# One softmax chain rewritten: queries times -1/8, the sink as one more column of the scores, a minimum for the maximum

## The chip, the core and the metric

The kernel runs on one core of a Trainium2 chip. The metric is the device time of one execution in microseconds (us); the time of a kernel is the median of its runs. The core has five engines with queues of their own: TensorE (PE in the profile, with its weight loads as PEld), VectorE (DVE), ScalarE (ACT), GpSimd (POOL) and SyncE (SP), which here issues most transfers.

## What is computed

One layer of a diffusion backbone on 1024 tokens of width 1024, with 256 context tokens: a modulated RMSNorm, then eight heads of windowed attention beside a short convolution, an output projection, and a mixture of 16 experts that each choose 128 tokens. The part that matters here is the attention's softmax, over one sink per head, all context keys and the keys within 128 positions:

```python
s_loc = jnp.einsum('bnqkgd,bnjkd->bnkgqj', qb, kb).astype(jnp.float32) * scale     # scale = 1/8
s_ctx = jnp.einsum('bnqkgd,bjkd->bnkgqj', qb, k_ctx).astype(jnp.float32) * scale
s_loc = jnp.where(valid[None, :, None, None], s_loc, -jnp.inf)
sk = jnp.broadcast_to(sink..., s_loc.shape[:-1] + (1,))
p = jax.nn.softmax(jnp.concatenate([sk, s_ctx, s_loc], axis=-1), axis=-1)
out = p_ctx @ v_ctx + p_loc @ v_loc        # the sink's share has no value
```

## The kernel before

All products that need precision are made of three: each operand is split into a high part (a cast on ScalarE) and a low part (a subtraction on VectorE or GpSimd).

The order of TensorE's instructions is the order in which the program writes them. For the other engines a planner chooses the order when the kernel is built, by a clock of its own; it may run an instruction long before the place where it is written. Some late parts of the kernel fix more engines by hand.

The stages in order: modulation and context; keys and values; the projection of the queries, tile by tile of 128 tokens (`q_proj`, line 496, and `q_turn`), woven with `mod_stream`, which sums further modulation rows on GpSimd; then the attention woven with the convolution; the output projection with the routing; the experts.

In `q_proj` a tile of queries is rotated (`rotary`, lines 328 to 335), split by L510 (high, ScalarE) and L511 (low, VectorE) into `qs`, and turned on TensorE in `q_turn` (L521).

The attention has 32 units: 8 blocks of 128 queries times 4 pairs of heads. `scores(u)` does a unit in two halves, one head each: two pairs of matmuls (L564 for the context keys, L566 for the window) into `ps_s`; one VectorE operation (L576) that adds the mask, writes the scores to `sm` in SBUF and gives the row's maximum with 8 times the sink (`sink8`) as the start; L578, that maximum times -1/8; and L579, the exponential on ScalarE with its sum `esum`. After the second half come the shares: L586 adds sink and negative maximum, L587 takes the exponential, L588 adds the sums, L589 takes the reciprocal for both heads at once, and the scores are multiplied by it, one head on ScalarE (L593) and one on VectorE (L595). A unit of blocks 1 to 6 has five key blocks (640 columns), one of blocks 0 and 7 four (512).

`values(u - 1)` is written between and behind the halves of `scores(u)`: it turns the shares of the unit before on TensorE, two key blocks at a time (L623), splits them (L626 high on ScalarE, L627 low on VectorE) and multiplies them with the values (L614). A unit of five key blocks has three such groups: two of 512 columns and one of 256. The last L614 of a unit need all of them. L640 and L644 take the result out.

The pair of score rows lies in one of the 21 slots of SBUF that the program hands out. During the attention the list of free slots is nearly empty, and the scores take turns in two of them, each free once the unit that held it has been turned.

The convolution's matmuls (L731 to L733) stand between those of the attention, three at a time. Beside them, ScalarE casts its weights (L711) and GpSimd subtracts (L712); and after a part of the convolution GpSimd multiplies (L756) and adds (L761, twice) the taps, which ScalarE scales (L760).

Of the kernel before, what the change touches and what calls it, by code (L numbers as in the profile page):

```python
# [9 lines left out]
F32 = mybir.dt.float32  # L10
# [3 lines left out]
AF = mybir.ActivationFunctionType  # L14
OP = mybir.AluOpType
# [6 lines left out]
NH = 8  # L22
# [4 lines left out]
NT = S // 128  # L27
# [3 lines left out]
NEG = -1.0e30  # L31
# [55 lines left out]
def tile_layer(ctx, tc, x, c, cx, c_ctx, w_ada, b_ada, g_mix, w_in, conv_w, sink, w_out, g_ffn,  # L87
               w_router, w_gate, w_up, w_down, g_final, rope, amask, ident_in, triu_in, iota_in, out):
    nc = tc.nc
    consts = ctx.enter_context(tc.tile_pool(name="consts", bufs=1))  # L90
# [5 lines left out]
    slots = Slots(big, NSLOT)  # L96
# [12 lines left out]
    def w4(name, shape=(1024,), dtype=F32, tag="w4"):  # L109
        return shaped(work.tile([128, 1026 if dtype != BF else 2052], dtype, tag=tag, bufs=NW4, name=name), shape)  # L110
# [4 lines left out]
    def p2(i, name):  # L115
        return psum.tile([128, 2, 512], F32, tag=f"P{i}", name=name)

    def p1(i, name):
        return psum.tile([128, 512], F32, tag=f"C{i}", name=name)
# [154 lines left out]
    sinkb = consts.tile([128, NH], F32, name="sinkb")  # L274
    sink8 = consts.tile([128, NH], F32, name="sink8")
    nc.sync.dma_start(sinkb, sink.partition_broadcast(128).rearrange("p o h -> p (o h)"))
    nc.vector.tensor_scalar(sink8, sinkb, 8.0, None, op0=OP.mult)

    def hT_slots(n, name):
        return [slots.get((4, n), F32R, name + a) for a in ("h", "l", "h", "l")]  # L280
# [19 lines left out]
    def hl(hT, k, tok):  # L300
        g, kk = divmod(k, 4)
        return hT[2 * g][0][:, kk, tok], hT[2 * g + 1][0][:, kk, tok]
# [193 lines left out]
    def q_proj(t):  # L496
        half, i = divmod(t, 4)
        ps = p2(1, "ps_q")[:, 0] if t % 2 else p1(3, "ps_q")
        for k in range(KC):
            hi, lo = hl(hT[half], k, slice(i * 128, (i + 1) * 128))  # L500
            g, kk = divmod(k, 4)
            mm(ps, hi, wq[g][0][0][:, kk], start=k == 0, stop=False)
            mm(ps, hi, wq[g][1][0][:, kk], start=False, stop=False)
            mm(ps, lo, wq[g][0][0][:, kk], start=False, stop=k == KC - 1)
            yield 0.65
        t1 = rotary([ps], t, 1, 8)

        qs = w4("qs", (8, 2, HD), F32R)
        tv = t1.rearrange("p (h d) -> p h d", d=HD)
        nc.scalar.copy(qs[:, :, 0, :], tv)  # L510
        nc.vector.tensor_tensor(qs[:, :, 1, :], tv, qs[:, :, 0, :].bitcast(F32), op=OP.subtract)  # L511
        qs_of[t] = qs

    def q_turn(t):
# [24 lines left out]


    attT = {}
    negm = consts.tile([128, NT, NH], F32, name="negm")
    mx = consts.tile([128, NT, NH], F32, name="mx")
    esum = consts.tile([128, NT, NH], F32, name="esum")
    rec = consts.tile([128, NT, NH], F32, name="rec")
    prob = {}

    def geometry(b):
        blocks = [t for t in (b - 1, b, b + 1) if 0 <= t < NT]
        return blocks, 128 * (2 + len(blocks))  # L550

    def scores(u):

        b, hp = divmod(u, 4)
        kv = hp // 2
        blocks, W = geometry(b)
        loc = slice(blocks[0] * 128, (blocks[-1] + 1) * 128)
        sm2, s_sm = slots.get((2, 640), F32, "sm")
        for i in range(2):
            h = 2 * hp + i  # L560
            ps = p2(0, "ps_s")
            st = qT[b // 2][0][:, b % 2, h]
            for a in range(2):
                mm(ps[:, 0, 256:512], st, KCx[:, a, kv, :], start=a == 0, stop=a == 1)  # L564
            for a in range(2):
                mm(ps[:, 1, 0:W - 256], st, KX[a][:, kv, loc], start=a == 0, stop=a == 1)  # L566
            sm = sm2[:, i, :W]
            src = ps.rearrange("p a b -> p (a b)")[:, 256:256 + W]
            dst = sm
            if b == 0:  # L570

                mk = maskt.rearrange("p (a b) -> p a b", a=2)[:, :, 0:256]
                dst, src = [v.rearrange("p (a b) -> p a b", a=2) for v in (sm, src)]
            else:
                mk = maskt[:, 0:W]
            nc.vector.tensor_tensor_reduce(dst, src, mk, op0=OP.add, op1=OP.max, scale=1.0,  # L576
                                           scalar=sink8[:, h:h + 1], accum_out=mx[:, b, h:h + 1])
            nc.vector.tensor_scalar(negm[:, b, h:h + 1], mx[:, b, h:h + 1], -0.125, None, op0=OP.mult)  # L578
            nc.scalar.activation(sm, sm, AF.Exp, bias=negm[:, b, h:h + 1], scale=0.125,  # L579
                                 accum_out=esum[:, b, h:h + 1])  # L580
            if i == 0:
                yield

        hs = slice(2 * hp, 2 * hp + 2)
        r = rec[:, b, hs]
        nc.vector.tensor_tensor(r, sinkb[:, hs], negm[:, b, hs], op=OP.add)  # L586
        nc.scalar.activation(r, r, AF.Exp)  # L587
        nc.vector.tensor_tensor(r, r, esum[:, b, hs], op=OP.add)  # L588
        nc.vector.reciprocal(r, r)  # L589
        for i in range(2):  # L590
            share = rec[:, b, 2 * hp + i:2 * hp + i + 1]
            if i:
                nc.scalar.activation(sm2[:, i, :W], sm2[:, i, :W], AF.Copy, scale=share)  # L593
            else:
                nc.vector.tensor_scalar(sm2[:, i, :W], sm2[:, i, :W], share, None, op0=OP.mult)  # L595
        prob[u] = (sm2, s_sm)
# [480 lines left out]
    i = todo.index(("g", NE - 1, 3))  # L1077
# [391 lines left out]
def _constants():  # L1469
    import ml_dtypes  # L1470
    t = np.arange(S)
    nf = HD // 4
    inv = (np.float32(10000.0) ** (-np.arange(nf, dtype=np.float32) / np.float32(nf))).astype(np.float32)
    ang = np.concatenate([(t // 64).astype(np.float32)[:, None] * inv, (t % 64).astype(np.float32)[:, None] * inv], -1)
    cs, sn = np.cos(ang).astype(np.float32), np.sin(ang).astype(np.float32)
    tab = np.stack([cs, sn, -sn], 1)
    rope = np.ascontiguousarray(tab.reshape(NT, 128, 3, 32).transpose(1, 0, 2, 3)).astype(np.float32)
    q = np.arange(128)[:, None]
    j = np.arange(128)[None, :]
    amask = np.zeros((128, 768), np.float32)  # L1480
    amask[:, 256:384] = np.where(j >= q, 0.0, NEG)
    amask[:, 512:640] = np.where(j <= q, 0.0, NEG)
    amask = amask.astype(ml_dtypes.bfloat16)
    ident = np.eye(128, dtype=np.float32)
    triu = np.triu(np.ones((128, 128))).astype(ml_dtypes.bfloat16)
    iota = np.concatenate([np.broadcast_to(np.arange(1, 129), (128, 128)),
                           np.arange(128)[:, None] + 128 * np.arange(NT)[None, :]], 1).astype(np.float32)
    return {"rope": rope, "amask": amask, "ident_in": ident, "triu_in": triu, "iota_in": iota}
# [28 lines left out]
```

## Time and profile before

| | us |
|---|---|
| median of 3 runs | 1169.38 |
| lowest and highest run | 1166.91, 1170.52 |
| the profiled execution | 1168.05 |
| its span, first to last instruction | 1166.3 |
| TensorE busy in it | 1061.0 (91%) |
| VectorE, ScalarE, GpSimd busy | 966.0, 765.4, 353.3 |

The span is read by stretches. From 110 to 177 us the queries are projected, from 177 to 418 us attention and convolution run together, from 442 us the output projection, from some 580 us the experts. The table by stretches gives each engine's busy time and the number of its instructions, then the granted clock, the share of time in which the transfer engines worked, and GB/s. The view in order of time gives start, length, engine, line, operation, output and inputs, shapes and count; behind it in brackets how long the engine had been idle and what ended that. A matmul's length reaches over the start of the next one, since they are pipelined.

### The profile page before, as it was taken

What the parts mean: (1) busy time and instruction counts of PE and PEld (TensorE: products, weight loads), DVE (VectorE), ACT (ScalarE), POOL (GpSimd) and SP (SyncE); (2) the same over time, 40 slices, a digit from 0 to 9 for tenths busy, and PEclk for the clock granted to TensorE, in tenths of its full rate; (3) what the DMA queues carried; (4) which work ended last, traced back from release to release, by engine and by line L of the source; (5) the groups of instructions that cost most, each with busy time, mean ns of one, the idle gap of its engine ahead of it and who ended that gap; (6) DMA issues with size and microseconds to landing.
All of it is one profiled execution on the core that took longest, in us unless ns stands there. A gap on an engine that the chain in (4) does not pass through costs nothing.

```text
span 1166.3 us, 15621 instructions
## 1 busy us (share of the span) xinstructions
PE 1061.0 (91%) x5486; PEld 875.6 (75%) x5486; DVE 966.0 (83%) x1661; ACT 765.4 (66%) x1057; POOL 353.3 (30%) x294
## 2 busy tenths in 40 slices
PE   6787889999899998998299999999999999999982
PEld 2675667888788877887188888888888888888861
DVE  7787455887878785489889999999999999999975
ACT  7566655766666743222178788778788778888853
POOL 0457681312203131221303333313333312330022
PEclk9797999999999998999599999999999999999996
DMA  9644540100101188657589999999999999999555
GB/s 375 231 163 144 164 145 20 37 19 1 55 1 37 31 307 293 163 142 267 225 295 353 410 393 390 391 390 387 407 394 387 390 391 386 403 398 391 219 182 233
DMA packets 90502, 291.84 MB, mean 250 GB/s; under 512 B 7012, under 2 KB 20784, under 8 KB 89400
## 3 DMA queue, kind: packets, MB, share of 16 engines
q1 hardware_dynamic: 84808, 270.40, 60.7%
q0 software_dynamic: 5616, 20.45, 7.2%
q8 instruction: 43, 0.70, 0.2%
q14 instruction: 35, 0.29, 0.1%
HBM read 266.69 MB, written 24.13 MB: 249 GB/s over the span
## 4 chain that ended last, share of the span: by engine, by line
PE 71%; DVE 11%; DMA 7%; ACT 4%; issue 4%; POOL 2%; POOLq 0%; ACTq 0%; DVEq 0%; SPq 0%
PE pg L1284 14%; PE pu L1284 14%; PE py L1284 13%; PE po L879 6%; PE ps_cv L732 3%; PE ps_cv L731 3%; PE ps_cv L733 3%; PE pt L623 2%; PE po_att L614 2%; DMA xt<-in_x_dram 2%; PE ps_s L566 2%; PE xTp L1270 1%; DVE whl L1133 1%; PE ps_s L564 1%; PE hTtp L1270 1%
## 5 line engine op out<-in xcount | busy, mean ns | idle before, releaser
L1133 DVE TENSOR_TENSOR whl<-raw,whl 128x1024 fp32r<-128x1024 f32 x384 | 455.2, 1224 | 30.5 <-ACT whl L1130 19.6
L1130 ACT CAST whl<-raw 128x1024 fp32r<-128x1024 f32 x384 | 400.2, 1054 | 101.1 <-PE pu L1284 35.7
L1284 PE MATMUL pg<-whl,xT 128*128 128x512 f32 x768 | 187.1, 396 | 2.1 <-DVE whl L1133 2.1
L1284 PE MATMUL pu<-whl,xT 128*128 128x512 f32 x768 | 180.9, 392 | 0.0
L1284 PEld LDWEIGHTS pg<-whl,xT 128*128 128x128 f32 x768 | 142.9, 189 | 31.9 <-DVE whl L1133 2.9
L1284 PE MATMUL py<-whl,hTt 128*128 128x512 f32 x720 | 165.8, 389 | 0.0
L1284 PEld LDWEIGHTS pu<-whl,xT 128*128 128x128 f32 x768 | 143.0, 188 | 29.5
L1284 PEld LDWEIGHTS py<-whl,hTt 128*128 128x128 f32 x720 | 135.1, 188 | 28.4 <-DVE whl L1133 0.3
L1249 POOL TENSOR_SCALAR oh<-iota,pos 128x128 bf16<-128x128 f32 x108 | 106.7, 1002 | 13.3 <-DVE pos L1234 12.8
L1342 POOL DMA_INDIRECT acc_d<-yt,idx x15 | 38.4, 2560 | 195.9 <-DVE yt L1330 195.9
L731 PE MATMUL ps_cv<-hTh,wcs 128*128 128x512 f32 x192 | 81.6, 425 | 0.0
L1294 POOL DMA_INDIRECT xr<-h_d,idx x16 | 21.7, 1357 | 188.8 <-DVE gate_w L1260 188.8
L464 POOL TENSOR_TENSOR acc<-acc,wmod 128x1024 f32<-128x1024 f32 x28 | 69.4, 2494 | 26.4 <-ACT wmod L462 25.9
L626 ACT CAST pth<-pt 128x512 fp32r<-128x512 f32 (+1 forms) x88 | 46.1, 524 | 46.3 <-PE pt L623 46.2
L733 PE MATMUL ps_cv<-hTh,wcs 128*128 128x512 f32 x192 | 76.3, 397 | 0.0
L732 PE MATMUL ps_cv<-hTl,wcs 128*128 128x512 f32 x192 | 76.2, 397 | 0.0
L879 PE MATMUL po<-woh,ah 128*128 128x512 f32 x240 | 71.3, 407 | 0.6 <-ACT woh L224 0.6
L627 DVE TENSOR_TENSOR pth<-pt,pth 128x512 fp32r<-128x512 f32 (+1 forms) x88 | 53.9, 613 | 20.1 <-ACT pth L626 19.2
L712 POOL TENSOR_TENSOR wcs<-wcr,wcs 128x1024 fp32r<-128x1024 f32 x12 | 28.6, 2389 | 110.0 <-ACT wcs L711 87.4
L579 ACT ACTIVATE sm<-sm,negm 128x640 f32<-128x640 f32 (+1 forms) x64 | 51.6, 807 | 4.4 <-DVE negm L578 4.3
L576 DVE CUSTOM_DVE_ANT_0 sm<-ps_s,maskt,sink 128x640 f32<-128x640 f32 (+1 forms) x56 | 48.3, 863 | 6.9 <-PE ps_s L566 6.3
L879 PEld LDWEIGHTS po<-woh,ah 128*128 128x128 f32 x240 | 44.6, 193 | 9.5 <-ACT woh L224 1.0
(285 smaller groups left out, 1821.6 us busy)
## 6 DMA issues: line engine op xcount, KB each, us to landing
raw<-in_w_gate_dram SPq DMA_DIRECT2D x64, 1024.0 KB, 10.1
raw<-in_w_up_dram SPq DMA_DIRECT2D x64, 1024.0 KB, 8.1
raw<-in_w_down_dram SPq DMA_DIRECT2D x64, 1024.0 KB, 10.4
wmod<-in_w_ada_dram SPq DMA_DIRECT2D x32, 512.0 KB, 3.8
wa<-in_w_ada_dram SPq DMA_DIRECT2D x8, 1024.0 KB, 9.5
wcr<-in_w_in_dram SPq DMA_DIRECT2D x12, 512.0 KB, 4.2
xt<-in_x_dram SPq DMA_DIRECT2D x4, 1024.0 KB
wor<-in_w_out_dram SPq DMA_DIRECT2D x4, 1024.0 KB
```

The source lines that it names most:

```text
L464: nc.gpsimd.tensor_tensor(acc, acc, wt, op=OP.add)
L576: nc.vector.tensor_tensor_reduce(dst, src, mk, op0=OP.add, op1=OP.max, scale=1.0, scalar=sink8[:, h:h + 1], accum_out=mx[:, b, h:h + 1])
L579: nc.scalar.activation(sm, sm, AF.Exp, bias=negm[:, b, h:h + 1], scale=0.125, accum_out=esum[:, b, h:h + 1])
L627: nc.vector.tensor_tensor(pth[:, 1, :n], pt[:, :n], pth[:, 0, :n].bitcast(F32), op=OP.subtract)
L731: mm(ps, wsp[:, 0, k], hi, start=k == 0, stop=False)
L732: mm(ps, wsp[:, 0, k], lo, start=False, stop=False)
L733: mm(ps, wsp[:, 1, k], hi, start=False, stop=k == KC - 1)
L879: mm(po[n], a, wo[k // 4, n][j][:, k % 4], start=first, stop=last)
L1130: nc.scalar.copy(w[:, 0], t[:, k % 2])
L1133: low = nc.vector.tensor_tensor(w[:, 1], t[:, k % 2], w[:, 0].bitcast(F32), op=OP.subtract)
L1249: nc.gpsimd.tensor_scalar(oh[:, t], iota1, pos[:, t, 0, e:e + 1], None, op0=OP.is_equal)
L1284: mm(ps[n], a_hl[:, a, k], w[:, j, n * 512:(n + 1) * 512], start=first, stop=last)
```

## The change

The queries are multiplied by -1/8 when they are split, so that the matmuls give the negative of the scaled scores. The masked places get a large positive number, the reduction takes the minimum and starts from minus the sink, and its result is the bias of the exponential as it stands (factor -1). The sink is one more column of the scores: GpSimd copies minus the sink of both heads behind the last column before the reduction, and the exponential and its sum take that column along. So the sum is the whole denominator: L578, L586, L587 and L588 go, and the reciprocal reads `esum`. The slot's rows are 648 long instead of 640.

```diff
-    nc.vector.tensor_scalar(sink8, sinkb, 8.0, None, op0=OP.mult)
+    nc.vector.tensor_scalar(sink8, sinkb, -1.0, None, op0=OP.mult)
...
-        nc.scalar.copy(qs[:, :, 0, :], tv)
-        nc.vector.tensor_tensor(qs[:, :, 1, :], tv, qs[:, :, 0, :].bitcast(F32), op=OP.subtract)
+        nc.scalar.activation(qs[:, :, 0, :], tv, AF.Copy, scale=-0.125)
+        nc.vector.scalar_tensor_tensor(qs[:, :, 1, :], tv, -0.125, qs[:, :, 0, :].bitcast(F32), op0=OP.mult,
+                                       op1=OP.subtract)
...
-        sm2, s_sm = slots.get((2, 640), F32, "sm")
+        sm2, s_sm = slots.get((2, 648), F32, "sm")
+        nc.gpsimd.tensor_copy(sm2[:, :, W], sink8[:, 2 * hp:2 * hp + 2])
...
-            nc.vector.tensor_tensor_reduce(dst, src, mk, op0=OP.add, op1=OP.max, scale=1.0,
+            nc.vector.tensor_tensor_reduce(dst, src, mk, op0=OP.add, op1=OP.min, scale=1.0,
                                            scalar=sink8[:, h:h + 1], accum_out=mx[:, b, h:h + 1])
-            nc.vector.tensor_scalar(negm[:, b, h:h + 1], mx[:, b, h:h + 1], -0.125, None, op0=OP.mult)
-            nc.scalar.activation(sm, sm, AF.Exp, bias=negm[:, b, h:h + 1], scale=0.125,
+            sx = sm2[:, i, :W + 1]
+            nc.scalar.activation(sx, sx, AF.Exp, bias=mx[:, b, h:h + 1], scale=-1.0,
                                  accum_out=esum[:, b, h:h + 1])
...
-        r = rec[:, b, hs]
-        nc.vector.tensor_tensor(r, sinkb[:, hs], negm[:, b, hs], op=OP.add)
-        nc.scalar.activation(r, r, AF.Exp)
-        nc.vector.tensor_tensor(r, r, esum[:, b, hs], op=OP.add)
-        nc.vector.reciprocal(r, r)
+        nc.vector.reciprocal(rec[:, b, hs], esum[:, b, hs])
...
-    amask[:, 256:384] = np.where(j >= q, 0.0, NEG)
-    amask[:, 512:640] = np.where(j <= q, 0.0, NEG)
+    amask[:, 256:384] = np.where(j >= q, 0.0, -NEG)
+    amask[:, 512:640] = np.where(j <= q, 0.0, -NEG)
```

## Rows read from the trace of the kernel before

**Rows 1.** The page's chain that ended last: shares of the span by engine.

```profile
PE 71%; DVE 11%; DMA 7%; ACT 4%; issue 4%; POOL 2%; POOLq 0%; ACTq 0%; DVEq 0%; SPq 0%
```

**Rows 2.** The table by stretches: the attention with the convolution, in one row.

```profile
177.00:418.00 241.00, 233.67 (x1402) 201.47 (x1403) 184.42 (x503) 160.71 (x342) 48.20 (x20) 0.99 0.12 37
```

**Rows 3.** In order of time: one quiet unit of five key blocks, second half.

```profile
259.21 0.60 PE L623 MATMUL pt<-ident,sm 128*128 128x128 f32 x4
...
259.52 0.08 DVE L576 DVE_READ_ACCUMULATOR2_ANT mx<- 128x1 f32 x1
...
259.64 0.15 DVE L578 TENSOR_SCALAR negm<-mx 128x1 f32<-128x1 f32 x1
...
259.84 0.59 ACT L626 CAST pth<-pt 128x512 fp32r<-128x512 f32 x1 [0.95 <-PE pt L623]
...
260.32 0.83 ACT L579 ACTIVATE sm<-sm,negm 128x640 f32<-128x640 f32 x1
...
260.46 0.69 DVE L627 TENSOR_TENSOR pth<-pt,pth 128x512 fp32r<-128x512 f32 x1 [0.48 <-ACT pth L626]
...
261.06 0.19 ACT L579 ACTIVATION_READ_ACCUMULATOR sm<-sm,negm 128x1 f32 x1
261.15 0.19 ACT L587 ACTIVATE rec<-rec 128x2 f32<-128x2 f32 x1
261.24 0.36 ACT L626 CAST pth<-pt 128x256 fp32r<-128x256 f32 x1
...
261.37 0.16 DVE L588 TENSOR_TENSOR rec<-rec,esum 128x2 f32<-128x2 f32 x1 [0.22 <-ACT rec L587]
...
261.57 0.17 DVE L589 RECIPROCAL rec<-rec 128x2 f32<-128x2 f32 x1
261.65 0.41 DVE L627 TENSOR_TENSOR pth<-pt,pth 128x256 fp32r<-128x256 f32 x1
261.74 0.87 PE L614 MATMUL po_att<-pth,vx 128*128 128x256 f32 x6
261.83 0.83 ACT L593 ACTIVATE sm<-sm,rec 128x640 f32<-128x640 f32 x1 [0.23 <-DVE rec L589]
```

**Rows 4.** In order of time: two of the long L586 and L588, and matmuls kept waiting.

```profile
232.67 1.36 DVE L586 TENSOR_TENSOR rec<-sinkb,negm 128x2 f32<-128x2 f32 x1
...
234.43 0.39 PE L614 MATMUL po_att<-pth,vx 128*128 128x256 f32 x1 [0.76 <-DVE pth L627]
...
290.29 2.37 POOL L761 TENSOR_TENSOR cg<-cg,tap 128x1024 f32<-128x1024 f32 x1
290.35 2.33 DVE L588 TENSOR_TENSOR rec<-rec,esum 128x2 f32<-128x2 f32 x1
...
293.61 0.79 PE L623 MATMUL pt<-ident,sm 128*128 128x128 f32 x4 [1.45 <-DVE sm L595]
...
376.27 0.39 PE L614 MATMUL po_att<-pth,vx 128*128 128x256 f32 x1 [0.94 <-DVE pth L627]
```

**Rows 5.** In order of time: the unit in which L595 ran ahead of L627.

```profile
336.03 0.55 DVE L595 TENSOR_SCALAR sm<-sm,rec 128x640 f32<-128x640 f32 x1
...
336.50 0.42 DVE L627 TENSOR_TENSOR pth<-pt,pth 128x256 fp32r<-128x256 f32 x1
...
336.98 0.38 PE L614 MATMUL po_att<-pth,vx 128*128 128x256 f32 x1 [0.19 <-DVE pth L627]
```

**Rows 6.** Groups by line and shape, ScalarE: total and mean ns; L510, L593.

```profile
L510 ACT CAST qs<-t 128x512 fp32r<-128x512 f32 x8 | 5.0, 623 | 15.8 <-DVE t L335 15.8
...
L593 ACT ACTIVATE sm<-sm,rec 128x512 f32<-128x512 f32 x8 | 5.8, 724 | 4.3 <-DVE rec L589 4.3
```

**Rows 7.** In order of time: GpSimd before the attention, an operation written at line 995.

```profile
175.21 0.25 POOL L995 CAST vals<-tokid 128x16 bf16<-128x16 f32 x1
```

**Rows 8.** In order of time: a share on VectorE beside a GpSimd operation.

```profile
219.15 2.87 POOL L756 TENSOR_SCALAR cg<-u,smallT 128x1024 f32<-128x1024 f32 x1 [19.00 <-DVE rec L588]
219.55 1.06 DVE L595 TENSOR_SCALAR sm<-sm,rec 128x640 f32<-128x640 f32 x1
```

More of the change, by code (lines that the diff above doesn't have):

```diff
@@ L541, in tile_layer @@
     attT = {}
-    negm = consts.tile([128, NT, NH], F32, name="negm")
     mx = consts.tile([128, NT, NH], F32, name="mx")
```

## The prediction

> **What bounds the kernel now.** I read the chain of waits first, then the table by stretches, then the order of time within one unit of the attention. The chain lies on TensorE for 71% of the span [rows 1]. The change touches two stretches, the query projection (110 to 177 us) and the attention woven with the convolution (177 to 418 us). In the second TensorE is busy 233.67 of 241 us, VectorE 184.42, ScalarE 160.71, GpSimd 48.20 [rows 2]. So all that could be won there is the 7.3 us in which TensorE idles, plus a little at each restart. A softmax operation on VectorE or ScalarE that runs beside the matmuls is worth nothing by its own length; it counts only where a matmul waits behind it.
>
> One quiet unit shows how close that is [rows 3]. While unit u's scores become shares, unit u-1's shares are turned, copied to a high part (L626, ScalarE) and a low part (L627, VectorE), and multiplied (L614). I call the three pairs of a unit a, b and c; c is the short one, and only units of five blocks have it (24 of 32). The sixth matmul of the last L614 group starts some 0.6 us after 261.74, at 262.33, and needs the low part of c, which is ready at 261.65 + 0.41 = 262.06. That is 0.27 us of room in each unit, 0.22 after some 0.05 for the signal (L626 c ends at 261.60 and L627 c starts at 261.65).
>
> **The change, part by part.**
> *Three little VectorE operations and one on ScalarE go.* Per unit two of L578 (0.15 us each), L586 and L588 (0.16 each) and L587 (0.19) [rows 3]: 0.62 us on VectorE, 0.19 on ScalarE, 20 and 6 us over 32 units. All of it lies beside matmuls, so as work it brings nothing.
>
> *Stalls in which L586 or L588 sat go or move.* Both read two operands of two columns, yet one took 1.36 us and one 2.33; the second ended as GpSimd's 2.37 us addition ended that had begun 0.06 us before it (290.29) [rows 4]. Nine such blocks, of 0.6 us and more, stand in the stretch, three on L586 and six on L588. TensorE idled 0.76 us behind the L586 one (through L627), 1.45 behind the 2.33 us one (through the share L595), 0.94 at 376.27 (through L627 again) [rows 4]. Without L586 its stall goes: 0.76 plus some 0.2 for the restart, 0.9 us. For the six L588 blocks the question is what VectorE does next. The share L595 takes 0.55 us for 640 columns [rows 5], and beside a GpSimd operation it once took 1.06 [rows 8], so it too is held up; what the block gave L588 it can give L595. If L627 stands ahead of L595 as now, L627 is freed; if not, nothing is won.
> The Trainium skill (SBUF — State Buffer, section on the two separate sides) says that a VectorE operation that uses both ports, or has two SBUF inputs, and a GpSimd operation shut each other out for the whole instruction. By that rule L595 would have waited until 222.02 and then run; it ended at 220.61, so the trace agrees that it is slowed and not that it waits for the end. By the rule rival A below wins 0.9 us through L595; by the row, where the hold-up was 0.5 us, some 1.5 us more, 1163.4.
>
> *The order on ScalarE and VectorE.* TensorE's order is written by hand; the order of the others is the planner's. It takes what is ready on its own clock: the little GpSimd operations of line 995, written far below, ran at 175.21 because they were ready [rows 7]. Of two that are ready I take it to prefer the one written first. Now follow the quiet unit [rows 3]. The second reduction's maximum is out at 259.52 + 0.08 = 259.60. Today L578 makes the exponential ready at about 259.83, just as L626 b is (259.84), and L626 b goes first. Without L578 the exponential is ready at about 259.65, 0.19 before it, on a ScalarE that sits idle (0.95 us before L626 b). Two ends:
>
> End 1, the exponential still goes second. It ends at 261.15. L626 c follows at once and ends at 261.51, so L627 c is ready at about 261.56. But the reciprocal L589 now needs only the sum read out at 261.25: it runs 261.30 to 261.47, and L595 is ready then, 0.1 us before L627 c. L595 goes first, to 262.01, and L627 c ends at 262.05 + 0.41 = 262.46 where 262.28 was wanted: 0.17 us lost per unit.
>
> End 2, the exponential goes first, 259.65 to 260.48. L626 b ends at 261.07 (now 260.43). L589 and L595 run on VectorE from 260.6 to 261.35, ahead of L627 b, which ends at 262.04. At 261.07 ScalarE finds the share L593 and L626 c both ready; L593 is written first and takes 0.83, so L626 c ends at 262.26 and L627 c at 262.71: 0.43 us lost per unit.
>
> The trace has one unit with L595 ahead of L627 c, at 336: the low part came at 336.92 and the sixth matmul started at 336.98, after 0.19 us of idle [rows 5]. So the price is real, and 0.19 lies nearer to the first end; the second end stands on an order that the trace does not show. I take 0.3, the middle: 24 x 0.3 = 7.2 us (4.1 to 10.3).
>
> *The sink as a column.* One GpSimd copy of 2 columns per unit; a GpSimd operation of 16 columns took 0.25 us [rows 7], so 32 of them are 8 us at most on an engine that is idle 80% of the stretch. The two slots of scores alternate, so it can start once c of the unit before has been turned, by 261.24 in the quiet unit, and the exponential needs it after the next scores (they follow the L614 of 262.33) and their reduction, near 264 by my estimate: 2.8 us of lead. One GpSimd operation of 2.87 us [rows 8] ahead of it is covered, to a tenth. The exponential has one column more of 640: nothing. The minimum in place of the maximum and the turned masks: the same operation, nothing.
>
> *The queries.* L510 becomes an activation with a factor. An activation of 512 columns with a factor takes 724 ns (L593), the cast 623 [rows 6]: 0.1 us for each of 8 tiles, between the rotation and the transposes that TensorE waits for; where GpSimd holds L511 up anyhow it is hidden. 0.4 of 0.8 us. L511 keeps two inputs and a result of the same size: nothing.
>
> *Sum.* 7.2 + 0.4 - 0.9 = +6.7 us. The work after 418 us hangs on the attention's last matmuls, and the stages behind it are TensorE's, so a shift is passed on. The profiled execution took 1168.05 us (span 1166.3, 1.75 around it): 1174.8. The median of the runs lies 1.33 above that execution: **1176.0 us**.
>
> **The rivals.**
> *A. The order holds, and the blocks are won (faster).* If the planner's clock has L627 c ready before L595, each unit keeps its room. Then the stalls behind L627 go: 0.76 and 0.94 [rows 4] and two more of about that size, 3.2 us, with 0.2 each for the restart 4.0; those through L595 shrink by the 0.3 us of L588 and L589 in three places, 0.9; less 0.4 for the queries: -4.5, 1164.9. For it: the present order has L627 c before L595 in the quiet unit and some twenty like it. Against: there L595 was not ready yet, because L587 and L588 (0.35 us and their signals) stood before it. It decides at 0.1 us.
> *B. Order holds or nearly, and the blocks only move to L595.* Only L586's 0.9 is won, against 0.4 and a few light stalls: 1168 to 1171.
> *C. The copies queue badly on GpSimd.* Three tap sequences fall into the stretch, each 2.87 us and two additions like the 2.37 us one [rows 4, 8], 7.6 us without their waits. A copy behind a whole sequence comes 7.6 - 2.8 = 4.8 us late, three times: +14, 1184. It decides from a delay of 2.8 us on. Against: the planner fits small ready operations into gaps [rows 7].
> *D. The stages behind take it up.* A shift of 1 to 3 us either way is lost in the loads of the output weights: within 0.3%.
>
> **How the numbers follow.** 0.3%, 3.5 us, is about what a measurement of this kernel can tell from no change. Forecast 0.53 (its lower end, +3.6, just touches the bound: slower 0.47, same 0.06); A 0.24 (faster 0.21, same 0.03); B 0.12 (same); D 0.06 (same); C 0.05 (slower). Faster 0.21, same 0.27, slower 0.52. The range reaches from A's time, 1165, to the second end with the queries at their dearest, 1169.4 + 10.3 + 0.8 = 1180.5, so 1181; it leaves out C and about half of A. The forecast's own range is 1173 to 1181.
>
> **What would show it.** In a quiet unit of the changed kernel: L595 ahead of L627 c (and in the second end the exponential ahead of L626 b, L593 ahead of L626 c); the time from one unit's scores to the next's longer by 0.17 to 0.43 us; TensorE's idle time in the stretch up from 7 to some 14 us, ended by L627. Long L586 and L588 are gone, and some L595 take 1 us or more. L510 stands at about 0.72. If the quiet units keep their length and L627 c still comes before L595, the forecast is wrong and A or B holds. If the exponential waits for GpSimd, C.

## The result and the profile after

The changed kernel takes 1179.78 us (median of 4 runs, 1175.91 to 1184.2) where the kernel before took 1168.91 beside it: a ratio of 1.0088, 95% interval 1.0067 to 1.011 (an estimate from all runs, not the quotient of the two medians). A second set of runs gave 1179.78 against 1170.44, 1.0082 [1.0063, 1.010]. The forecast was slower, 1176.0 in a range of 1165 to 1181. The profiled execution took 1176.65, its span is 1174.8: 8.5 more than the 1166.3 of before.

First where the time is. I cut both traces at three places: the first score matmul of the second unit, that of the 32nd unit, and the first matmul of the output projection (432.31 us before, 441.74 after). Between the first two lie **thirty units**: 217.39 us before, 224.30 after, so 6.9 of the 8.5 us arise there. The second unit starts 2.1 us later (187.43 against 185.29), from the 32nd unit to the output projection it is 0.4 more, and the stages behind it take 0.9 less. The 2.1 us can't be put down to the change: two executions of one and the same kernel further down (the old order) start their second unit at 189.73 and 187.69, and the kernel before with GpSimd's operations cut, whose query projection is that of before, at 187.95.

The page's first lines and the stretch that answers to [rows 2] (it begins with the first scores and ends some 12 us before the output projection, that of [rows 2] some 14 us before it; columns as there):

```profile
span 1174.8 us, 15543 instructions
## 1 busy us (share of the span) xinstructions
PE 1062.9 (90%) x5486; PEld 875.8 (75%) x5486; DVE 944.8 (80%) x1533; ACT 758.7 (65%) x1025; POOL 363.1 (31%) x326
...
179.30:430.00 250.70, 240.30 (x1414) 206.26 (x1415) 163.68 (x376) 154.44 (x310) 57.29 (x50) 0.99 0.12 38
```

VectorE has lost some 20 us of work, as the change intends, and TensorE idles 10.4 us in the stretch where it idled 7.3. In the thirty units alone it idles 8.8 instead of 6.0 us, and is counted busy for 215.5 instead of 211.4: part of the loss shows not as idle time but as longer groups of matmuls, such as the group of six below. Who ends TensorE's waits in the attention is told by the view of waits, 177 to 442 us (total us, times, longest):

```profile
PE po_att L612 <- DVE pth L625: 9.4, 10, 1.6
PE ps_s L567 <- DVE bias L490: 2.2, 1, 2.2
PE po_att L612 <- ACT pth L624: 0.5, 1, 0.5
```

The same view of before, 177 to 433 us:

```profile
PE po_att L614 <- DVE pth L627: 4.9, 8, 1.1
...
PE pt L623 <- DVE sm L595: 1.8, 2, 1.4
```

Before, the value matmuls waited 4.9 us for the low part in eight places, and the turning matmuls 1.8 us for the share L595. Now nearly all of it is the low part (L627 is L625 here, L626 is L624, the shares L595 and L593 are L593 and L591, the value matmuls L614 are L612).

One quiet unit in order of time, the second half, against [rows 3]:

```profile
267.24 0.08 DVE L579 DVE_READ_ACCUMULATOR2_ANT mx<- 128x1 f32 x1
...
267.36 0.83 ACT L582 ACTIVATE sm<-sm,mx 128x641 f32<-128x641 f32 x1 [0.82 <-DVE mx L579]
...
268.19 0.84 ACT L624 CAST pth<-pt 128x512 fp32r<-128x512 f32 x2
...
268.32 0.17 DVE L587 RECIPROCAL rec<-esum 128x2 f32<-128x2 f32 x1 [0.99 <-ACT sm L582]
268.52 0.55 DVE L593 TENSOR_SCALAR sm<-sm,rec 128x640 f32<-128x640 f32 x1
...
268.68 0.44 POOL L561 COPY sm<-sink 128x2 f32<-128x2 f32 x1 [7.17 <-DVE rec L587]
...
268.92 0.84 ACT L591 ACTIVATE sm<-sm,rec 128x640 f32<-128x640 f32 x1
268.99 1.01 DVE L625 TENSOR_TENSOR pth<-pt,pth 128x512 fp32r<-128x512 f32 x2
...
269.46 0.99 PE L612 MATMUL po_att<-pth,vx 128*128 128x256 f32 x6
```

The exponential follows its minimum at once and goes ahead of high b. High b and high c run as one group (x2). VectorE takes reciprocal and share L593 first, and the low parts of **both** b and c come behind them (x2, 268.99 to 270.0). The group of six value matmuls lasts 0.99 instead of 0.87: the quiet unit is 7.08 us long where it was 6.95.

Then one unit in which GpSimd is at work, against [rows 4]:

```profile
304.15 2.40 POOL L759 TENSOR_TENSOR cg<-cg,tap 128x1024 f32<-128x1024 f32 x1 [2.66 <-ACT tap L758]
...
304.91 0.17 DVE L587 RECIPROCAL rec<-esum 128x2 f32<-128x2 f32 x1 [1.11 <-ACT sm L582]
305.11 1.79 DVE L593 TENSOR_SCALAR sm<-sm,rec 128x640 f32<-128x640 f32 x1
...
305.93 0.40 PE L612 MATMUL po_att<-pth,vx 128*128 128x256 f32 x2
306.49 0.45 POOL L561 COPY sm<-sink 128x2 f32<-128x2 f32 x1
306.82 1.01 DVE L625 TENSOR_TENSOR pth<-pt,pth 128x512 fp32r<-128x512 f32 x2
...
307.55 0.74 PE L612 MATMUL po_att<-pth,vx 128*128 128x256 f32 x4 [1.22 <-DVE pth L625]
```

A hold-up of a VectorE operation by GpSimd is called a block, as in the prediction. The share of 0.55 us takes 1.79: it ends 0.35 us after GpSimd's addition (304.15 + 2.40 = 306.55). Behind it stand both low parts, and TensorE waits 1.22 us for the first of them. Five such shares of 1.76 to 1.81 us stand in the attention. So the blocks did what the prediction asked about: they moved from L586 and L588 to the share, and what they hold up now is what TensorE needs next.

Taken unit by unit, after less before over the thirty: fifteen units are 0.06 to 0.24 us longer, most of them 0.13 (1.9 in all), nine are 0.35 to 2.2 longer (6.9), the rest are no longer or shorter (-1.9). Two of the nine hold a share of 1.76 us or more (200.76, 321.23); the units of 305.11 and 382.24 had held a long L588 before and are no longer than they were, and the fifth (417.21) stands in the 32nd unit. Others of the nine hold an operation that the old order had room for: in the unit at 255.88 ScalarE's copy for the convolution (0.58 us, before high b) comes ahead of the exponential, and the unit is 0.39 longer. The rest of the nine were not taken apart.

The two smaller parts of the change: the queries' high part, by line and shape from 110 to 182 us, against [rows 6], and the copy of the sink in the view of the tile `sm` (shortest, median and longest in ns):

```profile
L511 ACT ACTIVATE qs<-t 128x512 fp32r<-128x512 f32 x8 | 5.1, 634 | 21.8 <-DVE t L335 21.8
...
L561 POOL COPY sm<-sink x31: 186/406/649, 177.5 to 409.7; 128x2 f32<-128x2 f32 x31
```

### The profile page after: what moved, and what is told of

The parts are those of the page before. It is cut to its first block, busy times and chain, and to the rows that moved or that the text cites. A ratio compares the mean times of both kernels' runs of the same rounds, so it can differ in the third digit from the quotient of the medians.

```text
span 1174.8 us, 15543 instructions
## 1 busy us (share of the span) xinstructions
PE 1062.9 (90%) x5486; PEld 875.8 (75%) x5486; DVE 944.8 (80%) x1533; ACT 758.7 (65%) x1025; POOL 363.1 (31%) x326
## 4 chain that ended last, share of the span: by engine, by line
PE 71%; DVE 12%; DMA 6%; issue 5%; ACT 4%; POOL 2%; POOLq 0%; ACTq 0%; DVEq 0%; SPq 0%
PE pg L1282 15%; PE pu L1282 14%; PE py L1282 13%; PE po L877 6%; PE ps_cv L729 2%; PE ps_cv L730 2%; PE ps_cv L731 2%; PE po_att L612 2%; PE pt L621 2%; DMA xt<-in_x_dram 2%; PE ps_s L569 1%; PE xTp L1268 1%; DVE whl L1131 1%; PE ps_s L567 1%; PE hTtp L1268 1%
## 5 line engine op out<-in xcount | busy, mean ns | idle before, releaser
L582 ACT ACTIVATE sm<-sm,mx 128x641 f32<-128x641 f32 (+1 forms) x64 | 51.7, 808 | 25.1 <-DVE mx L579 25.1
L624 ACT CAST pth<-pt 128x512 fp32r<-128x512 f32 (+1 forms) x88 | 43.9, 521 | 31.9 <-PE pt L621 31.7
L625 DVE TENSOR_TENSOR pth<-pt,pth 128x512 fp32r<-128x512 f32 (+1 forms) x88 | 52.2, 611 | 12.9 <-ACT pth L624 12.7
L561 POOL COPY sm<-sink 128x2 f32<-128x2 f32 x32 | 10.9, 340 | 138.0 <-PE pt L621 66.4
```

The lines of the kernel that those rows point to most:

```text
L582: nc.scalar.activation(sx, sx, AF.Exp, bias=mx[:, b, h:h + 1], scale=-1.0, accum_out=esum[:, b, h:h + 1])
L625: nc.vector.tensor_tensor(pth[:, 1, :n], pt[:, :n], pth[:, 0, :n].bitcast(F32), op=OP.subtract)
```

## The experiments

"Thirty units" is the stretch above, taken from each trace; a repeated kernel gave 212.31 and 212.34, another 224.30 and 224.50, so 0.2 us is about what it can tell. The median is that of all runs, and the ratio with its interval is against the kernel before on the same chip. In the order "old", the share on VectorE stands behind the last low part and the second exponential behind high b. That is how they stand in 30 of the 31 units with a unit before them in the kernel before; in the changed kernel the exponential goes ahead of high b and the share ahead of low b in 27 of 31.

| kernel | thirty units | median | before beside it | ratio [95%] |
|---|---|---|---|---|
| before | 217.39 | 1168.91 | | |
| after | 224.30 | 1179.78 | 1168.91 | 1.0088 [1.0067, 1.011] |
| after, again | 224.50 | 1179.78 | 1170.44 | 1.0082 [1.0063, 1.010] |
| after, old order | 212.31 | 1164.69 | 1169.98 | 0.9945 [0.9926, 0.9964] |
| after, old order, again | 212.34 | 1165.82 | 1170.63 | 0.9952 [0.9934, 0.9970] |
| after, only the share held | 214.89 | 1166.67 | 1169.98 | 0.9962 [0.9948, 0.9976] |
| after, only the exponential held | 217.46 | 1177.41 | 1169.98 | 1.0051 [1.0032, 1.0070] |
| before, queries scaled | 217.35 | 1169.93 | 1169.98 | 1.0000 [0.9989, 1.0010] |
| before, sink as a column | 217.38 | 1169.36 | 1170.44 | 0.9993 [0.9980, 1.0005] |
| after, sink's own chain back | 222.66 | 1175.78 | 1170.44 | 1.0037 [1.0024, 1.0051] |
| after, old order, GpSimd cut | 211.50 | 1170.29 | 1170.44 | 0.9997 [0.9982, 1.0012] |
| after, GpSimd cut | 218.46 | 1175.96 | 1170.63 | 1.0049 [1.0030, 1.0068] |
| before, GpSimd cut | 211.45 | 1166.96 | 1170.63 | 0.9963 [0.9946, 0.9979] |

**The theory** was that the new order on ScalarE and VectorE makes the change slow, and that the work it takes out is a gain. **The rivals**: the loss comes from the sink's column and its copies on GpSimd, from the queries, or from the blocks that GpSimd causes, whatever the order.

### The old order put back

The changed kernel, with the second exponential written behind high b and the shares behind the last pair; `only_after` fixes an order on one engine and adds no wait between engines.

```diff
+            high = nc.scalar.copy(pth[:, 0, :n], pt[:, :n])
+            low = nc.vector.tensor_tensor(pth[:, 1, :n], ...)
...
+            if j0 == 2 and "exp" in late:
+                only_after(late.pop("exp")(), high)
+            if j0 + 2 >= nb and "shares" in late:
+                late.pop("shares")(low)
```

In `shares(low)` stands `only_after(share on VectorE, low)`.

> The changed kernel with the old order put back: the second exponential of a unit stands behind the second high part (512 columns) on ScalarE, and both shares behind the last low part on VectorE. Theory O (the loss of the attention stage comes from the order in which shares and exponentials run ahead of the copies that matmuls wait for): units without a neighbour on GpSimd come back from some 7.1 us to 6.95, no matmul waits for the low parts of 256 columns in them, and the attention stage ends at least 9 us earlier than in the changed kernel: 1164 to 1169 us, about as before or faster, with the 2 us of the query stage still lost. Rival P (the loss comes from the port that VectorE's share and GpSimd dispute, and from the 32 copies on GpSimd): order alone helps little, 1174 us or more.

Measured: 1164.69 us, 0.9945 [0.9926, 0.9964], faster than both kernels; the repetition on another chip:

> The changed kernel in the old order of ScalarE and VectorE once more, beside the two others. Theory: 1163 to 1167 us again, below the kernel before by 0.4 to 0.7%. If it comes out level with the kernel before, the first result was one of the chip it ran on.

It gave 1165.82, 0.9952 [0.9934, 0.9970]. The thirty units are 5.1 us shorter than before and 12.0 shorter than in the changed kernel. One quiet unit in order of time, where L591 is the exponential, L647 and L648 the high and low part, L609 the share:

```profile
262.74 0.59 ACT L647 CAST pth<-pt 128x512 fp32r<-128x512 f32 x1 [1.01 <-PE pt L644]
...
263.22 0.84 ACT L591 ACTIVATE sm<-sm,mx 128x641 f32<-128x641 f32 x1
263.36 0.69 DVE L648 TENSOR_TENSOR pth<-pt,pth 128x512 fp32r<-128x512 f32 x1 [0.86 <-ACT pth L647]
...
264.44 0.42 DVE L648 TENSOR_TENSOR pth<-pt,pth 128x256 fp32r<-128x256 f32 x1
264.63 0.87 PE L635 MATMUL po_att<-pth,vx 128*128 128x256 f32 x6
264.78 0.54 DVE L609 TENSOR_SCALAR sm<-sm,rec 128x640 f32<-128x640 f32 x1
```

The group of six is back at 0.87, the quiet unit at 6.95. Blocked shares are still there, and one is longer than any of after, but what waits behind it is not due yet:

```profile
293.08 2.38 POOL L786 TENSOR_TENSOR cg<-cg,tap 128x1024 f32<-128x1024 f32 x1
293.15 2.67 DVE L609 TENSOR_SCALAR sm<-sm,rec 128x640 f32<-128x640 f32 x1
...
295.96 0.63 PE L644 MATMUL pt<-ident,sm 128*128 128x128 f32 x4 [1.00 <-DVE sm L609]
```

2.1 us of hold-up cost TensorE 1.00 here, where 1.24 cost it 1.22 in the changed kernel. The waits of this kernel, in the stretch from 181 to 432 us, against the 9.4 us of after (1.9 of the 2.1 lie behind the thirty units):

```profile
PE po_att L635 <- DVE pth L648: 2.1, 2, 1.9
PE pt L644 <- DVE sm L609: 1.5, 2, 1.0
```

So the order is the cause, and the removed operations are a gain of 5.1 us where the order is kept. The gain sits where the blocks were: six units in or just behind a long L586 or L588 are 5.9 us shorter than before, one later unit is 1.0 longer, and the others differ by 0.2 at most. That the order is now held in all 31 units instead of 30 is worth 0.2 of it (the unit at 329.7, of [rows 5]).

### Half of the order each

Only the shares held behind the low part of c; and only the exponential held behind high b, with the share free to go ahead of low c.

Both against the kernel with the old order; first the exponential set free:

```diff
-            if i and u and True:
+            if i and u and False:
```

> The changed kernel with the shares alone held behind the last low part; the exponential may still go ahead of the second high part. Theory O, with the shares as the main cause: the last low part is ready some 0.4 us earlier than in the changed kernel, quiet units at 6.95 to 7.0 us, 1165 to 1171 us. If the exponential that goes ahead is the main cause instead, quiet units stay at 7.1 us and the time at 1174 us or more.

Then the shares set free:

```diff
-            if j0 + 2 >= nb and "shares" in late:
-                late.pop("shares")(low)
+            if j0 == 2 and "shares" in late:
+                late.pop("shares")()
```

> The changed kernel with the second exponential alone held behind the second high part; the shares come when they are ready, ahead of the last low part of 256 columns. By the first end of the prediction: 0.17 us lost per unit of five blocks, quiet units at 7.1 us, 1172 to 1177 us. If the exponential is the main cause: 6.95 us and 1165 to 1170 us.

The share held alone takes back 9.4 of the 12.0 us (214.89), the exponential alone 6.8 (217.46). They overlap, since an exponential that goes second also brings low b out ahead of the share. The second kernel has the prediction's End 1: exponential second, share ahead of low c alone. Its quiet units are 7.14 us long, 0.19 more than the old order's. Its median, 0.4 us above the range expected, is higher than its attention explains, by a stage that the change doesn't touch: behind the last expert's first matmuls the span takes 83.0 us instead of 77.4. In that stretch TensorE waits for ScalarE's split of the expert weights, which it doesn't do in the kernel before:

```profile
PE py L1471 <- ACT whl L1155: 3.7, 1, 3.7
```

The planner laid out the tail in another order as well. The kernel with the sink's own chain, below, shows it too (82.2 us).

### The parts alone

Only the queries, on the kernel before (times +1/8, the other factors taken back):

```diff
-        nc.scalar.copy(qs[:, :, 0, :], tv)
-        nc.vector.tensor_tensor(qs[:, :, 1, :], tv, ..., op=OP.subtract)
+        nc.scalar.activation(qs[:, :, 0, :], tv, AF.Copy, scale=0.125)
+        nc.vector.scalar_tensor_tensor(qs[:, :, 1, :], tv, 0.125, ..., op0=OP.mult, op1=OP.subtract)
```

> The kernel before with the queries alone scaled (by +1/8) when they are split; the reduction, the sink's chain and all operations of the attention stay, with the factors 1 in place of 1/8 and 8. If the 2.2 us by which the attention starts later in the changed kernel come from the scaled split: the attention starts 2 us later than before and the whole takes 1170 to 1172 us. If they are luck of the alignment with GpSimd's additions or come with other parts of the change: the start moves by under 0.6 us, 1169 to 1170 us.

Nothing: ratio 1.0000 [0.9989, 1.0010], thirty units 217.35. The attention does start later than before (its first scores 3.9 us, its second unit 2.4 us, at 187.64), as the first of the two readings expected, but so it does in the kernel with the split of before and GpSimd cut (2.7 us, at 187.95), and the whole takes no longer: the output projection starts 2.5 us later than before, the first expert at 579.26 in both. The queries are no part of the loss.

Only the sink's column, on the kernel before (L578 stays, the exponential takes the column along):

```diff
+        nc.gpsimd.tensor_copy(sm2[:, :, W], sink8[:, 2 * hp:2 * hp + 2])
...
-        (L586, L587, L588 and the old reciprocal)
+        nc.vector.reciprocal(rec[:, b, hs], esum[:, b, hs])
```

> The kernel before with the sink as one more column alone: the operation that turns the maximum into the bias stays (L578 in the kernel before), the queries are not scaled, the sink's own chain of an addition, an exponential and an addition goes. Theory O says that it is this chain whose loss lets VectorE's share run ahead of the last low part, so the loss is here already: quiet units at some 7.1 us, the attention stage 2 us or more longer than before, 1171 to 1178 us. Rival: the lost bias operation (the exponential ahead of the second high part) is the cause: 1168 to 1170 us, quiet units at 6.95.

No difference that can be told, 0.9993 [0.9980, 1.0005], and not because nothing happens. In one of its units (L588 the reciprocal, L594 the share, L626 the low part of c):

```profile
269.12 0.17 DVE L588 RECIPROCAL rec<-esum 128x2 f32<-128x2 f32 x1
...
269.32 0.55 DVE L594 TENSOR_SCALAR sm<-sm,rec 128x640 f32<-128x640 f32 x1
...
269.59 1.05 PE L613 MATMUL po_att<-pth,vx 128*128 128x256 f32 x6
269.79 0.42 DVE L626 TENSOR_TENSOR pth<-pt,pth 128x256 fp32r<-128x256 f32 x1
```

Again End 1: the share goes ahead of low c, the group of six takes 1.05, 0.18 more, and sixteen units are longer by some 0.19 each, 3.0 us. Five other units give 3.4 us back; in or just behind four of them L586 or L588 had been held before. So the quiet units came as the theory expected (7.1) and the time as its rival did: a gain and a loss of one size. The arrangement and the thirty units are those of the kernel with the exponential alone held (217.46). Copies of two columns on GpSimd in all 32 units made nothing slower that the trace shows.

The other part alone: the minimum as the bias, no L578, but the sink added by its own chain (L585, exponential, L587):

```diff
-        nc.vector.reciprocal(rec[:, b, hs], esum[:, b, hs])
+        nc.vector.tensor_tensor(r, sinkb[:, hs], mx[:, b, hs], op=OP.add)
+        nc.scalar.activation(r, r, AF.Exp)
+        nc.vector.tensor_tensor(r, r, esum[:, b, hs], op=OP.add)
+        nc.vector.reciprocal(r, r)
```

> The changed kernel with the sink's own chain put back (addition, exponential, addition, reciprocal) and no sink column: what remains is the minimum that serves as the bias as it stands, without the operation between, and the scaled queries. Theory O with the shares as the cause: the share still waits for the chain and comes behind the last low part, quiet units stay at 6.95 us, 1167 to 1171 us. Rival (the exponential that runs ahead is the cause): quiet units at 7.1 us, 1172 us or more.

1.0037 [1.0024, 1.0051], and 5.3 us more in the thirty units: taking out an operation of 0.15 us (with the queries scaled, which alone cost nothing) makes the attention slower. The median alone would not show it, since the longer tail of 82.2 us stands in it too. Its quiet units are 6.97 to 7.00, as the theory expected, but the time is the rival's (1172 or more): the loss is not in the quiet units. It is in units like this one:

```profile
319.63 2.38 POOL L711 TENSOR_TENSOR wcs<-wcr,wcs 128x1024 fp32r<-128x1024 f32 x1 [7.91 <-ACT wcs L710]
319.82 2.21 DVE L585 TENSOR_TENSOR rec<-sinkb,mx 128x2 f32<-128x2 f32 x1
...
321.95 1.01 DVE L626 TENSOR_TENSOR pth<-pt,pth 128x512 fp32r<-128x512 f32 x2
...
322.68 0.74 PE L613 MATMUL po_att<-pth,vx 128*128 128x256 f32 x4 [1.29 <-DVE pth L626]
```

The exponential goes first here too, so low b and low c both stand behind L585, and L585 waits for GpSimd. It is the same pattern as in the changed kernel, with another operation in the share's place. So each of the two losses turns one order round: without the sink's chain the share goes ahead of low c, without L578 the exponential goes ahead of high b, and without both the share goes ahead of low b too.

### GpSimd's operations cut into four

If the blocks are what the order is costly for, shorter GpSimd operations should take the cost away. The weight subtraction and the three tap operations were cut into four parts of 256 columns, in the old order, in the changed kernel and in the kernel before.

```diff
-        nc.gpsimd.tensor_tensor(wsp[:, 1], raw, wsp[:, 0].bitcast(F32), op=OP.subtract)
+        for q in range(4):
+            ks = slice(2 * q, 2 * q + 2)
+            nc.gpsimd.tensor_tensor(wsp[:, 1, ks], raw[:, ks], wsp[:, 0, ks].bitcast(F32), op=OP.subtract)
...
-                    nc.gpsimd.tensor_tensor(y, y, tap, op=OP.add)
+                    for q in range(4):
+                        nc.gpsimd.tensor_tensor(y[:, cs], y[:, cs], tap[:, cs], op=OP.add)
```

> The changed kernel with the old order put back, and GpSimd's operations of 1024 columns beside the attention (the subtraction of the convolution's weights, the taps) in four parts of 256 columns each. If VectorE's share waits for the GpSimd operation that runs when it comes, and no longer, the shares of 1.3 to 2.7 us of the restored order shrink to 0.5 us plus one quarter, 1.2 us at most, the matmuls behind them wait less, and the time is 1161 to 1164.5 us. If a share that is held up waits until GpSimd is idle, the long shares stay and the time is as with the restored order, 1164 to 1166 us.

> The changed kernel with GpSimd's weight subtraction and tap operations cut in four parts of 256 columns each; the order on VectorE and ScalarE is left as the change made it. The attention stage of the changed kernel took 262.4 us, of the changed kernel in the old order 250.5. Theory (two terms: some 0.13 us in each of 24 quiet units, 3.1 us, and the rest, about 9 us, from VectorE shares held for up to 1.8 us by a GpSimd operation with the low parts queued behind them): no share over 1.1 us is left, quiet units stay near 7.08, the attention falls to 253 to 256 us. Rival (the order costs what it costs in every unit, long shares or not): the attention stays at 260 to 263.

> The kernel before with the same cut of GpSimd's operations. It shows what the cut is worth and costs by itself. Attention stage before: 255.15 us with nine operations of two columns held up for 0.6 to 2.3 us. Theory: those shrink, the attention falls to about 250 to 252; if the cut costs time outside the attention (as the kernel with both the old order and the cut suggests, 1170.3 against 1164.7 us), the median is still 1168 to 1171; if it doesn't, about 1166.

The thirty units stand in a table of two by three:

| thirty units, us | GpSimd whole | cut in four |
|---|---|---|
| chain of before | 217.39 | 211.45 |
| changed chain, old order | 212.31, 212.34 | 211.50 |
| changed chain, the planner's order | 224.30, 224.50 | 218.46 |

The cut takes 5.9 us from the kernel before, the change in the old order takes 5.1, and both together 5.9: they remove the same stalls. The change as it stands costs 6.9 us against before with whole operations and 7.0 with cut ones. My expectation for the changed kernel with the cut was an attention of 253 to 256 us (from the first scores to the output projection); it was 254.93, so the number held. The kernel before with the cut took 249.11, 0.9 less than the least expected. The reasoning behind it held by half: the long shares are gone (none above 1.08 us), the order still costs 7.0, and quiet units explain some 2.3 of that. A row of that kernel shows the rest (317 us, GpSimd's four parts shown as one line):

```profile
317.03 3.07 POOL L712 TENSOR_TENSOR wcs<-wcr,wcs 128x256 fp32r<-128x256 f32 x4 [6.60 <-ACT wcs L709]
...
318.01 0.81 DVE L593 TENSOR_SCALAR sm<-sm,rec 128x640 f32<-128x640 f32 x1
318.74 1.01 DVE L625 TENSOR_TENSOR pth<-pt,pth 128x512 fp32r<-128x512 f32 x2
...
319.47 0.74 PE L612 MATMUL po_att<-pth,vx 128*128 128x256 f32 x4 [0.67 <-DVE pth L625]
```

A hold-up of a mere 0.26 us in front of the low parts is a wait of 0.67 on TensorE: it comes on top of the room that the order has used up, and of a high b that the exponential made late.

By the whole time the cut is worth less than its 5.9 us: the kernel before with it is at 0.9963 [0.9946, 0.9979]. In the stretch from the output projection to the first expert the three cut kernels take 150.7, 151.5 and 150.7 us, the kernel before 148.7 (the other kernels 146.2 to 149.0). TensorE waits there 4.3 to 5.7 us for the low part of the output weights (L225) where it waited 2.9 before: some of what the attention wins is lost again in a stage behind it. In the old order with the cut the shares are as short as expected (1.06 us at most), but neither of the two times expected came: nothing is left in the median (1170.29, 0.9997), although its profiled execution (1167.68) has the short attention; its runs spread from 1166.67 to 1173.73, and what the long ones lose no profile shows. That stays open.

The changed kernel was also run again beside these:

> The changed kernel itself, unchanged, on the same chip as the three beside it, so that they can be compared with it directly. Both theories: 1176 to 1183 us, quiet units at some 7.1 us.

## Why the prediction was right, and where only its sum was

**The direction and the place were right.** 6.3 us were forecast for the attention (7.2 - 0.9), 6.9 measured in the thirty units; 6.7 for the whole, 8.6 between the two profiled executions, 2.1 of it from a start that varies as much (2.0) between two executions of one kernel. The step behind it, that without L578 and L586 to L588 the exponential and the share are ready earlier and go ahead of high and low parts, is what the trace shows, and the old order put back takes it away. The median lies 3.1 us above the profiled execution, more than the 1.33 I took from the kernel before; what the longer executions lose is not in a profile.

**The price of the order was mis-sized, and so was what the blocks give; the errors cancel.** I set +7.2 for the order and -0.9 for the blocks. Measured against the old order, the planner's order costs 12.0 (224.30 less 212.3), and the removed operations give 5.1 (217.39 less 212.3). That +6.9 comes so close to +6.3 is luck.
- The price in a quiet unit: End 1's 0.17 was 0.19 where its arrangement appeared (the sink's column alone). End 2's 0.43 was 0.13. There high c did not wait for the share on ScalarE: I had taken the planner to prefer the operation written first, and it took high c (one group with high b at 268.19) before L591 (268.92), which is written first.
- Missing from 7.2 was the product of order and blocks. I treated a blocked share as something from which "nothing is won". With low b and low c behind it, it loses: 1.22 us of TensorE's time in the row at 307.55. With GpSimd cut the order costs 7.0 (218.46 less 211.50), so some 5.0 of the 12.0 are this product. The 7.0 is not the 7.2 of the sum either: its quiet units make 2.3. The sentence that was right ("what the block gave L588 it can give L595") needed a second half: who stands behind L595 now.
- The blocks' gain was put at 0.9, as if only L586's stall could go. With the order kept it is 5.1; rival A had it at 4.0 and 0.9 together, 4.9.

**The hold-up by GpSimd.** I read it from [rows 8], the share beside a multiplication with one input (L756), where it took 1.06. The blocks were beside operations of two inputs (L712, L761), and there the share is held till the end: in the six cases after in which it took longer than alone, it ends 0.28 us (512 columns) or 0.35 us (640) behind GpSimd's operation. The Trainium skill (SBUF — State Buffer, section on the two separate sides) says that a VectorE operation that uses both ports is shut out for the whole of GpSimd's instruction. These six rows agree with it, where I had followed the row; that the share uses both ports no run shows. The nearest row was one of another kind.

**The queries** were put at 0.4 us: an activation with a factor 0.1 us dearer than a cast, from L593 at 724 ns [rows 6]. L593's factor is one number per partition, read from SBUF. With a constant factor L511 took 634 ns against 623, 0.09 us over the eight tiles, and the queries alone gave 1.0000. The term can't be told from 0.

**The copies and the other rivals.** No exponential of the changed kernel waited for GpSimd, and the sink's column alone cost nothing beyond the order: rival C falls. Rival A fell for the kernel as it is, and its time is that of the changed kernel in the old order: 1164.9 forecast, 1164.69 and 1165.82 measured. Rival B's way, the blocks moving to the share, happened, at a higher price than it had set. Rival D did not decide: of the 9.4 us by which the output projection starts later, the stages behind it take up 0.9. A shift of the size that D names was taken up whole, though, in the kernel with the queries scaled (2.5 us).

**The sign shown for each step.** Quiet units 0.13 longer (0.17 to 0.43 forecast), share ahead of low c: yes; TensorE's idle time up to 10.4 (14 forecast); long shares in place of long L586 and L588: yes; L510 at 0.72: no, 0.63.

## What to carry to other kernels

Taking an operation out of a chain makes what follows ready earlier. Where a planner or a queue takes what is ready, look first at what the earlier operation will pass on its engine, and whether TensorE needs that next; if so, fix the order along with the change, as here, where the same edit is 0.9% slower in one order and 0.5% faster in the other. An operation that another engine can hold up belongs behind the ones that are due, not in front of them; and a bound for a hold-up is read from a row in which the same kinds of operations meet.

## What the runs showed of the hardware that was not expected

The share on VectorE (one input and a result in SBUF, 640 columns, 0.55 us alone) is held up by GpSimd in two ways. Beside an operation of two inputs that starts first it ends 0.28 (512 columns) to 0.36 us after that has ended. Beside the tap multiplication of one input it ends long before that, as in [rows 8] and here:

```profile
224.11 2.86 POOL L754 TENSOR_SCALAR cg<-u,smallT 128x1024 f32<-128x1024 f32 x1 [0.58 <-DVE rec L587]
224.58 0.99 DVE L593 TENSOR_SCALAR sm<-sm,rec 128x640 f32<-128x640 f32 x1
```

It ended 1.46 us after GpSimd's start, at 225.57. In [rows 8] it was 1.46 too, and in the old order, the sink's column and the share held alone 1.45 to 1.47, wherever the share had begun. VectorE's additions of two columns show when the hold-up ends. One in the kernel before, then a share in the kernel with the sink's own chain back:

```profile
287.36 2.85 POOL L756 TENSOR_SCALAR cg<-u,smallT 128x1024 f32<-128x1024 f32 x1 [19.37 <-DVE u L739]
...
288.20 0.28 DVE L586 TENSOR_TENSOR rec<-sinkb,negm 128x2 f32<-128x2 f32 x1
```

```profile
221.33 3.02 POOL L755 TENSOR_SCALAR cg<-u,smallT 128x1024 f32<-128x1024 f32 x1 [18.65 <-DVE u L738]
...
222.90 0.55 DVE L594 TENSOR_SCALAR sm<-sm,rec 128x640 f32<-128x640 f32 x1
```

The addition of 0.16 us ended 1.12 us after GpSimd's start; the share that began 1.57 us after it took its 0.55, though GpSimd's operation had 1.45 us to go. By the Trainium skill (SBUF — State Buffer, section on the two separate sides) the lock lasts for the whole instruction; here VectorE was let in 1.1 us into an instruction of 2.9 to 3.0, and why isn't known. The reciprocal (0.17 beside GpSimd at 304.91 as at 268.32 without it) and the low parts, which read one input from PSUM (1.01 for two beside GpSimd at 318.74, as at 268.99 beside none of its long operations), were not held up. The hold-up works the other way as well: GpSimd's copy of two columns took 0.19 us in most units of the old order and 0.44 where it began during a share (268.68).
